# Dilated attention's projections: token order of the stationary operand and of the rows kept in DRAM

## The chip, the cores and the metric

The kernel runs on one core of a Trainium2 chip. The metric is the device time of one execution in microseconds. Three runs of the kernel before took 3687.85, 3690.18 and 3696.85 us, with a median of 3690.18 us.

## The reference

A first block (a modulated mixer with a bidirectional mLSTM and an MLP) is followed by a second block of two layers. The change lies in the second block. There, each layer normalises 1024 tokens of 1024 features, multiplies them by a wide matrix and feeds three branches: a recurrent mixer (RWKV), a sparse attention that chooses 256 keys for each query, and a dilated attention. The results go through an output matrix and a gated per-layer input. The dilated branch:

```python
DIL_WINDOWS = (128, 512, 2048)
DIL_RATES = (1, 4, 16)

def dilated_group(q, k, v, rate, steps):
    B, S, H, dh = q.shape
    n = S // rate
    to_res = lambda t: jnp.swapaxes(t.reshape(B, n, rate, H, dh), 1, 2).reshape(B * rate, n, H, dh)
    o, lse = banded_attention(to_res(q), to_res(k), to_res(v), steps)
    o = jnp.swapaxes(o.reshape(B, rate, n, H, dh), 1, 2).reshape(B, S, H, dh)
    lse = jnp.swapaxes(lse.reshape(B, rate, n, H), 1, 2).reshape(B, S, H)
    return o, lse

def dilated_branch(z, cos, sin):
    q, k, v, g = split_cols(z, DIL_COLS)
    q = partial_rope(heads(q), cos, sin)
    k = partial_rope(heads(k), cos, sin)
    for gi in range(DIL_GROUPS):          # two heads of 64 in each of three groups
        o, lse = dilated_group(q[:, :, hs], k[:, :, hs], v[:, :, hs], DIL_RATES[gi], DIL_WINDOWS[gi] // DIL_RATES[gi])
        ...
    alpha = jax.nn.softmax(jnp.stack(lses, axis=2), axis=2)
    return (o * alpha).reshape(B, S, DIL_WIDTH) * jax.nn.silu(g)
```

So group 0 attends over neighbouring tokens, group 1 over tokens of the same class modulo 4, and group 2 over tokens of the same class modulo 16.

## The kernel before

The second block works on half-layers of 512 tokens, (layer 0, half 0), (0, 1), (1, 0) and (1, 1). For each, `in2` (line 1159) makes the projections, `branches` (line 1077) runs the sparse and the dilated attention, and `rwkv` (line 1527) the recurrent mixer in three units per half.

All projections use `dense` (line 273). The normalised tokens lie feature-major in SBUF as eight tiles of 128 features x 512 tokens, each split into a high part `xh` and a low part `xl`. Weights stream in, 256 columns and two k tiles at a time: `chunk` (line 248) loads 256 KB, ScalarE rounds them to `wh` (line 254), GpSimd takes the rest as `wl` (line 255), with three buffers of each. Each product is three matmuls, `wh` with `xh`, `wh` with `xl` and `wl` with `xh` (line 287). Two kinds exist:

- `dense_a` (line 298) makes feature-major results. The weights are the stationary operand and 512 tokens the moving one.
- `dense_b` (line 305) makes token-major results. 128 tokens are the stationary operand and 256 weight columns the moving one. Two token tiles share a PSUM bank, and a group of 256 columns fills two banks.

`in2` has seven groups of the second kind (`tok`, line 1179). Groups 0 to 3 hold the sparse attention's columns and group 0 of the dilated attention. They take tokens in natural order (`nat`) and are stored in a DRAM tensor `zd` of 512 x 1024. Groups 4 to 6 hold the queries, keys and values of the dilated groups 1 and 2. They take every fourth token (`cls`, line 1175), so that one token tile is one class modulo 4, and are stored in a DRAM tensor `zc` of four classes x 128 rows x 768 columns. ScalarE copies each bank to SBUF (line 1182), and SyncE's queue stores it (line 1183). In half 0 the order of the groups is 0, 3, 1, index keys in the first unit of the recurrent mixer, 2 and 4 in the second, 5, 6 and the gates in the third. In half 1 it is 0, 3, 1, index keys ahead of all, then 2 and 4, then 6 and 5, then the gates.

The dilated attention (`dil`, line 1726) has 12 blocks in each half, 3 groups x 4. For groups 1 and 2 a block is one class. `dil_keys` (line 1750) loads its queries and keys `zq` (line 1768), its values `dv` (line 1770) and, in half 1, the values of the half before (line 1774). GpSimd rotates `zq` by a table that is laid out by class. Scores, values and statistics go out by `dil_rows` (line 1747), which for groups 1 and 2 picks every fourth row of a DRAM tensor; `ud` and `ml` are written that way (lines 1829 and 1805).

The sparse attention chooses its keys in `choose` (line 1665), 31 steps of a sign count on ScalarE (line 1687), a count and small updates on VectorE (lines 1689 to 1692), one behind the other. It runs for the row tiles from the third of a layer on. The attention of a row tile (`dsa_attend`, line 1612) ends in a product with its gate, loaded from DRAM (lines 1621 and 1662).

Nothing is ordered by hand on the engines. A planner puts the instructions of each engine in order by a simulated timeline and by priorities: `branches` comes first, the recurrent mixer second, the projections fill in. Each engine, and SyncE's queue of DMAs, then runs its own order. All DMAs are issued by SyncE.

Of the kernel before, what the change touches and what calls it, by code (L numbers as in the profile page):

```python
# [15 lines left out]
PSUM = bass.MemoryType.PSUM  # L16
# [179 lines left out]

class K:
# [36 lines left out]
    def f(self, name):  # L234
        """a scratch tile of 2 KB a partition"""
        return self.fp.tile([128, 516], F32, name=name, tag="f", bufs=4)
# [5 lines left out]
    def chunks(self, src, n):  # L242
        """a group of n weight columns, split exactly into two float32r parts, two k tiles at a time"""
        nc = self.nc
        for j in range(0, src.shape[1], 2):
            yield self.chunk(src, n, j)
# [11 lines left out]
    def narrow(self, src, xs, out):  # L258
        """feature-major products of 64 columns, with the weights' two parts side by side: those of the second part
        come out from partition 64 on"""  # L260
        nc = self.nc
# [11 lines left out]
    def dense(self, src, n, banks):  # L273
        """products with a streamed weight group. banks: lists, one per PSUM bank, of (out, xs, f), where f makes
        (lhsT, rhs) of the weights and x of a k tile. Only a bank's first product starts its sums."""
        last = src.shape[1] - 1
        for ch in self.chunks(src, n):
            self.products(ch, banks, 0, last)
# [14 lines left out]
    def tok_jobs(self, ps, xs, t0, pick=None):  # L293
        """two token tiles of 256 columns in one bank"""
        pick = pick or (lambda x, t: x[:, 128 * t:128 * t + 128])
        return [(ps[:, 256 * t:256 * t + 256], xs, lambda w, x, t=t0 + t: (pick(x, t), w)) for t in range(2)]

    def dense_a(self, src, n, xs):
        """feature-major products [columns, 512] of a group of n weight columns, one bank per 128"""
        out = [self.bank(self.dense_tag()) for _ in range(0, n, 128)]  # L300
        self.dense(src, n, [[self.col_jobs(ps[:min(128, n - 128 * c)], xs, 128 * c, min(128, n - 128 * c))]
                            for c, ps in enumerate(out)])
        return out

    def dense_b(self, src, xs, pick=None, n=2):
        """token-major products of a group of 256 weight columns: n banks [128, 2 token tiles, 256]"""
        out = [self.bank(self.dense_tag()) for _ in range(n)]
        self.dense(src, 256, [self.tok_jobs(ps, xs, 2 * c, pick) for c, ps in enumerate(out)])
        return out
# [8 lines left out]
    def rsqrt(self, dst, v, n, tag=""):  # L318
        """dst = v ** -0.5 for small tiles, by Newton from a bit-level seed"""
# [13 lines left out]
    def ln_stats(self, src, eps):  # L333
        """src [128, 1024] -> (mean, rstd, -mean*rstd) columns"""
# [13 lines left out]
    def halves(self, n, pool=None, bufs=8):  # L348
        """the high and low parts of eight k tiles of n columns"""
# [5 lines left out]
    def make_xt(self, tiles, scale, bias=None, pool=None, tag="pt"):  # L355
        """normalised token tiles -> feature-major hi/lo parts, scaled and shifted per feature"""
# [92 lines left out]
    def ada_a(self, w0):  # L449
        nc, I = self.nc, self.I  # L450
        cT = self.v1["cT"]
        # silu(c) = (tanh(c/2) + 1) * c/2
# [6 lines left out]
        # 16 columns of each condition  # L459
# [13 lines left out]
    def ada_weights(self, g, pool=None):  # L473
        """the rows of a group of 256 modulation columns, by k"""
# [7 lines left out]
    def ada_rows(self, ps, g, pool):  # L482
        """256 columns: four partial sums over k, on 32 partitions each"""
# [4 lines left out]
    def ada_pair(self, g, pool=None):  # L488
        """feature-major shifts and scales of 512 columns; scales have their +1 in the bias"""
# [13 lines left out]
    def ada_row(self, dst, g0, g):  # L503
        """dst [128, 1024]: a column group of the modulation, the same in every partition"""
# [19 lines left out]
    def conv(self, j, raw, n, out):  # L524
        """taps over raw[:, 0:n+2], silu"""
# [10 lines left out]
    def inproj_a(self, h, tiles, ctiles=None):  # L536
        """q, k (convolved), values and gates of the context and of half 0; of half 1 the gates only"""
# [74 lines left out]
    def spread(self):  # L612
        """a piece of the modulation that later steps need"""
# [3 lines left out]
    def sg_prep(self):  # L617
        """weights of the spatial gating and its per-token offsets"""
# [12 lines left out]
    def uvo(self, h):  # L631
        """spatial gating branch and output gate of half h, kept in DRAM"""
# [41 lines left out]
    def gates(self):  # L674
        """mLSTM gate fields; rows 0..3 run forward, rows 32..35 backward (in flipped order)"""
# [75 lines left out]
    def mlstm_a(self):  # L751
        """states at the start of every latent chunk, both directions"""
# [31 lines left out]
    def mlstm_b(self):  # L784
        nc, pm, C = self.nc, self.pm, self.Cst
        H = []
        for l in range(8):
# [14 lines left out]
            for d in range(2):  # L802
# [10 lines left out]
                # weights are at most one where they count  # L813
# [38 lines left out]
            # head norm, output gate  # L852
# [28 lines left out]
    def load_yt(self, h, pool, th, tl, bufs):  # L881
        """the two mixer halves, feature-major, in hi/lo parts"""
# [19 lines left out]
    def deepnorm(self, z):  # L902
        """layer norm of a token tile [128, 1024], in place"""
# [76 lines left out]
    def consts2(self):  # L980
        """constants and vectors of block 2"""
# [6 lines left out]
        # 0, 1 and -1, and very low numbers  # L988
# [33 lines left out]
    def block2(self):  # L1022
# [16 lines left out]
        self.zd, self.zc, self.gd = d("zd", [512, 1024]), d("zc", [4, 128, 768]), d("gd", [5, 128, 512])  # L1039
# [37 lines left out]
    def branches(self, i, h):  # L1077
        """sparse and dilated attention of a half: a row tile's choice of keys runs beside the attention of the one before"""
# [27 lines left out]
    def square(self, x, out, ss):  # L1106
        """ss = sums of the squares of x"""
        self.nc.scalar.activation(out, x, AF.Square, accum_out=ss)

    def sums(self):  # L1110
        """room for the sums of squares of up to four token tiles, by groups of 256 columns"""
        return self.sm.tile([128, 4, 4], F32, name="rms_ss")

    def rms(self, ss, n):
        """[128, n]: 1 / (root mean square) of n token tiles"""
# [8 lines left out]
    def shift(self, i, j, ps, z):  # L1124
        """token-shift mix of one column tile"""
# [8 lines left out]
    def gate_out(self, i, h, j, ps):  # L1134
        """2 * silu of a gate tile, kept in DRAM"""
# [6 lines left out]
    def in2_prep(self, i, X, tag="pd", ss=None):  # L1142
        """the normalised rows of four token tiles, feature-major"""
# [15 lines left out]
    def in2(self, i, h, X, xs=None):  # L1159
# [14 lines left out]
        nat = lambda x, t: x[:, 128 * t:128 * t + 128]  # L1174
        cls = lambda x, j: x.rearrange("p (n j) -> p j n", j=4)[:, j]
        zd = self.zd[i, h].rearrange("(c t p) n -> c p t n", c=2, t=2)
        zc = self.zc[i, h].rearrange("(c t) p n -> c p t n", c=2)

        def tok(g, dst, pick, o):
            for c, ps in enumerate(self.dense_b(I["w2B"][i, g], xs, pick)):  # L1180
# [16 lines left out]
        def gates(g):  # L1197
            for c, ps in enumerate(self.dense_a(A[7 + g], 256, xs)):
                self.gate_out(i, h, 2 * g + c, ps)

        first = [lambda: tok(0, zd, nat, 0), lambda: tok(3, zd, nat, 256), lambda: tok(1, zd, nat, 768), index_keys]
        t2, t4, t5, t6 = (lambda: tok(2, zd, nat, 512), lambda: tok(4, zc, cls, 0), lambda: tok(5, zc, cls, 256),
                          lambda: tok(6, zc, cls, 512))
# [21 lines left out]
    def rope(self, x, heads, width, name, t):  # L1225
        """rotate the first 16 (or 8) columns of every head in place; x [128, heads * width]"""
# [14 lines left out]
    def rwkv_a(self, i, h, p, wd, zr, zk, zv, zg):  # L1241
        """six heads by pairs: head j of a pair lies on partitions 64 j to 64 j + 63. Decay, keys and rates of a pair"""
# [11 lines left out]
        # by chunks: rates, keys, and the second head's rates again  # L1254
# [8 lines left out]
        # normalised keys  # L1263
# [26 lines left out]
    def rwkv_b(self, i, h, p, PC, P, kk, BK, zr, kp, zv, zg):  # L1290
        """chunk products, and inverses of the unit lower triangles, by doubling"""
# [3 lines left out]
        # own: a head's partitions, other: its neighbour's  # L1295
# [11 lines left out]
        def products(q):  # L1307
            """of four chunks, by heads: rates and keys against A and R. Rates end up on the head's own partitions."""
# [25 lines left out]
        def token_major(q):  # L1334
            """of four chunks: minus the rates, and the keys"""
# [17 lines left out]
        # rows against U on a head's own partitions, against V on the other ones  # L1353
# [24 lines left out]
        # of T the first block of 32 is left to do  # L1378
# [11 lines left out]
        # the last level, by its blocks  # L1390
# [16 lines left out]
    def inverse16(self, L, T, TT):  # L1407
        """the blocks of 16 on the diagonals of the unit lower triangles inverted (T; TT is its transpose), by doubling.
        Through DRAM a block comes onto one partition."""
# [14 lines left out]
        def part(x, w, r, c):  # L1424
            """the quarters (r, c) of the diagonal blocks of 2 w of x [64, 16, 16]: [64, blocks, w, w]"""
# [3 lines left out]
        # the blocks' strict upper parts fill up; Y[:, 1] is the transpose  # L1429
# [24 lines left out]
    def rwkv_c(self, i, h, p, PC, AR, XB, YB, TT, W, KB, bv, sg):  # L1454
        """the chain over chunks, then group norm, bonus and gate"""
        nc = self.nc
        Z = self.layer[i]["Z"][p]
        # of the very last pair, the outputs of the first tokens don't wait for the others
# [4 lines left out]
        for c in range(8):  # L1463
            cs = slice(c * 64, c * 64 + 64)
            pz = self.bank("pc", 1)
            # a head's rows of W: the state, then U
# [30 lines left out]
    def rwkv_y(self, i, h, p, py, bv, sg, t0, t1, tag):  # L1497
        """group norm, bonus and gate of some chunks; the mean is out already"""
# [28 lines left out]
    def rwkv(self, *unit):  # L1527
        """the first part of a pair and the rest of the one before; without a pair the rest only"""
# [6 lines left out]
    def dsa_scores(self, i, h, t):  # L1535
        """keys and index scores of a row tile of 128; where all keys before a query count, 0 for these, else very low"""
# [18 lines left out]
        # queries: high and low parts against the high parts of keys; high against low  # L1555
# [16 lines left out]
        # indexer rows: high, low, high parts against high, high, low  # L1572
# [16 lines left out]
        # index scores  # L1589
# [22 lines left out]
    def dsa_attend(self, i, h, t, qT, acc):  # L1612
        """attention of a row tile over its chosen keys"""
# [51 lines left out]
    def choose(self, x, n):  # L1665
        """x [128, n] scores -> 0 for the 256 greatest of each row (of equal ones the first), -2^103 for the others.
# [334 lines left out]
```

## Time and profile before

| | |
|---|---|
| median of three runs | 3690.18 us |
| span of the profiled execution | 3684.1 us |
| TensorE matmul busy | 3446.7 us (94%), 24036 instructions |
| TensorE weight loads busy | 2953.4 us (80%) |
| VectorE busy | 2124.3 us (58%) |
| ScalarE busy | 1745.5 us (47%) |
| GpSimd busy | 1344.0 us (36%) |
| DMA | 376.61 MB, mean 102 GB/s |

The page gives no second time for the profiled execution, only its span from the first to the last instruction; the median of the runs is 6.1 us above that span. In the profile PE is TensorE's matmul, PEld its weight load, DVE is VectorE, ACT is ScalarE, POOL is GpSimd and SP is SyncE; a `q` behind the name is the engine's own queue of instructions that are not counted as busy. Matmuls are pipelined, so that the records of two of them overlap; the distance between two starts says how fast they follow.

### The profile page before, as it was taken

Reading aid. Unit: us, or ns where it says so; the run is one execution under the profiler, and the core shown is the slowest. Engines: PE = TensorE matmul, PEld = TensorE weight load, DVE = VectorE, ACT = ScalarE, POOL = GpSimd, SP = SyncE. Lnnn points to the kernel's source line nnn. Section 1 sums busy time; section 2 is a strip of 40 time slices with the busy share of each in tenths; the row PEclk is TensorE's granted clock in tenths of the full one; section 3 lists DMA queues with packets and bytes.
Section 4 is the critical chain, followed back from the end, with each engine's and each line's share of the span. In section 5 each row is a group of like instructions: output and inputs, shape, how many; then the busy total and the mean of one; then the engine's idle time right before and its main releaser. Section 6 shows DMA issues by size and latency. Waiting matters only on the chain. (4 is left out here: it accounts for less than half of the span.)

```text
span 3684.1 us, 66369 instructions
## 1 busy us (share of the span) xinstructions
PE 3446.7 (94%) x24036; PEld 2953.4 (80%) x24036; DVE 2124.3 (58%) x6359; ACT 1745.5 (47%) x3976; POOL 1344.0 (36%) x1331
## 2 busy tenths in 40 slices
PE   7989898999999989999999999899999999899897
PEld 5968787999899978887787787688888878688776
DVE  6277858112711264436655898872357555778974
ACT  3244334333333333337635666553357545557654
POOL 1333345444644463322322232233232233133245
PEclk8999998999999999998998899799999999899899
DMA  5433352222322233223321322332233432132434
GB/s 219 130 100 118 124 184 82 95 97 95 107 95 95 96 126 101 79 81 106 107 77 54 106 75 61 117 90 83 71 113 82 135 96 80 48 112 64 129 120 142
DMA packets 322856, 376.61 MB, mean 102 GB/s; under 512 B 113376, under 2 KB 189408, under 8 KB 322528
## 3 DMA queue, kind: packets, MB, share of 16 engines
q1 hardware_dynamic: 322528, 372.37, 32.4%
q8 instruction: 189, 3.10, 0.3%
q14 instruction: 139, 1.14, 0.1%
HBM read 315.54 MB, written 56.72 MB: 101 GB/s over the span
## 5 line engine op out<-in xcount | busy, mean ns | idle before, releaser
L255 POOL TENSOR_TENSOR wl<-wf,wh 128x512 fp32r<-128x512 f32 x812 | 1084.2, 1338 | 1835.0 <-ACT wh L254 1698.8
L254 ACT ACTIVATE wh<-wf 128x512 fp32r<-128x512 f32 x812 | 508.4, 627 | 903.4 <-PE pd L287 388.1
L287 PE MATMUL pd<-wh,xh 128*128 128x256 f32 x2240 | 699.8, 314 | 22.3 <-ACT raw L567 6.6
L287 PE MATMUL pd<-wh,xl 128*128 128x256 f32 x2240 | 695.1, 311 | 0.0
L287 PE MATMUL pd<-wl,xh 128*128 128x256 f32 x2240 | 692.7, 312 | 2.5 <-POOL wl L255 2.1
L287 PEld LDWEIGHTS pd<-wh,xh 128*128 128x128 f32 x2240 | 485.0, 217 | 42.9 <-issue 9.4
L287 PEld LDWEIGHTS pd<-wl,xh 128*128 128x128 f32 x2240 | 484.0, 217 | 16.4 <-issue 6.1
L287 PEld LDWEIGHTS pd<-wh,xl 128*128 128x128 f32 x2240 | 487.1, 217 | 9.9 <-issue 1.2
L287 PE MATMUL pd<-xh,wh 128*128 128x512 f32 x896 | 372.9, 417 | 28.8 <-DVE tg L1139 17.3
L287 PE MATMUL pd<-xl,wh 128*128 128x512 f32 x896 | 363.9, 406 | 0.2 <-DVE xl L371 0.2
L287 PE MATMUL pd<-xh,wl 128*128 128x512 f32 x896 | 352.7, 407 | 0.1
L1687 ACT ACTIVATE junk<-acc,t_nt 128x384 bf16<-128x384 f32 (+3 forms) x372 | 257.1, 691 | 145.7 <-DVE t_nt L1692 115.2
L287 PEld LDWEIGHTS pd<-xh,wh 128*128 128x128 f32 x896 | 175.4, 196 | 73.1 <-DVE tg L1139 18.3
L287 PEld LDWEIGHTS pd<-xl,wh 128*128 128x128 f32 x896 | 175.1, 195 | 39.3 <-issue 3.9
L287 PEld LDWEIGHTS pd<-xh,wl 128*128 128x128 f32 x896 | 174.2, 194 | 39.7 <-issue 1.7
L954 DVE CAST hh<-f 128x512 fp32r<-128x512 f32 x64 | 54.1, 845 | 243.2 <-ACT f L951 243.2
L1689 DVE TENSOR_SCALAR_CACHE_REDUCE junk<-acc,t_nt 128x384 bf16<-128x384 f32 (+2 forms) x186 | 125.5, 675 | 3.6
L1603 DVE SCALAR_TENSOR_TENSOR acc<-r,iw,acc 128x512 f32<-128x512 f32 (+3 forms) x140 | 102.8, 734 | 34.4 <-ACT r L1598 32.1
L1691 DVE TENSOR_SCALAR t_dec<-t_s,t_kb 128x1 int32<-128x1 f32 x372 | 77.8, 209 | 69.1 <-ACT junk L1687 64.7
L287 PE MATMUL pd<-wh,hh 128*128 128x256 f32 x384 | 108.7, 283 | 3.3 <-DVE y L923 3.3
L287 PE MATMUL pa<-wl,hh 128*128 128x256 f32 x384 | 108.0, 284 | 3.4 <-POOL wl L255 3.4
L287 PE MATMUL pb<-wh,hh 128*128 128x256 f32 x384 | 109.3, 285 | 0.2 <-ACT wh L254 0.2
(555 smaller groups left out, 7881.0 us busy)
## 6 DMA issues: line engine op xcount, KB each, us to landing
wf<-in_w_dram SPq DMA_DIRECT2D x256, 256.0 KB, 3.0
wf<-in_w2A_dram SPq DMA_DIRECT2D x144, 256.0 KB, 3.2
wf<-in_w2B_dram SPq DMA_DIRECT2D x112, 256.0 KB, 3.1
wf<-in_w_in_dram SPq DMA_DIRECT2D x80, 256.0 KB, 3.1
wf<-in_w2o_dram SPq DMA_DIRECT2D x80, 256.0 KB, 3.2
wf<-in_w2g_dram SPq DMA_DIRECT2D x80, 256.0 KB, 3.1
wa<-in_w_ada_dram SPq DMA_DIRECT2D x32, 512.0 KB, 5.1
X<-x_d SPq DMA_DIRECT2D x20, 512.0 KB, 5.1
```

Of the source, the lines that this page charges most:

```text
L254: nc.scalar.activation(wh, wf, AF.Copy)
L255: nc.gpsimd.tensor_sub(wl, wf, wh.bitcast(F32))
L287: self.nc.tensor.matmul(out, lhsT, rhs, start=k == first and j == 0 and q == 0, stop=k == last and j == len(bank) - 1 and q == 2)
L954: nc.vector.tensor_copy(hh, f)
L1603: nc.vector.scalar_tensor_tensor(a, r[:, :n], iw[:, hd:hd + 1], a, op0=OP.mult, op1=OP.add)
L1687: nc.scalar.activation(junk[:, :m], x[:, :m], AF.Sign, scale=-1.0, bias=nt, accum_out=s)
L1689: ts(junk[:, m:], x[:, m:], nt, 0.0, op0=OP.is_le, op1=OP.add, accum_out=c0)
L1691: ts(dec, s, kb, 2.0 ** b, op0=OP.is_lt, op1=OP.mult)
```

## The change

`tok_jobs` and `dense_b` lose their `pick`, and all seven groups take tokens in natural order. `zc` becomes 512 rows x 768 columns in natural order. `dil_keys` picks its class from it when it loads, by `dil_rows`, as every fourth row. The rest of the diff takes out comments and docstrings.

```diff
-    def tok_jobs(self, ps, xs, t0, pick=None):
-        pick = pick or (lambda x, t: x[:, 128 * t:128 * t + 128])
-        return [(ps[:, 256 * t:256 * t + 256], xs, lambda w, x, t=t0 + t: (pick(x, t), w)) for t in range(2)]
+    def tok_jobs(self, ps, xs, t0):
+        return [(ps[:, 256 * t:256 * t + 256], xs, lambda w, x, t=t0 + t: (x[:, 128 * t:128 * t + 128], w))
+                for t in range(2)]
...
-        self.dense(src, 256, [self.tok_jobs(ps, xs, 2 * c, pick) for c, ps in enumerate(out)])
+        self.dense(src, 256, [self.tok_jobs(ps, xs, 2 * c) for c, ps in enumerate(out)])
...
-        self.zd, self.zc, self.gd = d("zd", [512, 1024]), d("zc", [4, 128, 768]), d("gd", [5, 128, 512])
+        self.zd, self.zc, self.gd = d("zd", [512, 1024]), d("zc", [512, 768]), d("gd", [5, 128, 512])
...
-        nat = lambda x, t: x[:, 128 * t:128 * t + 128]
-        cls = lambda x, j: x.rearrange("p (n j) -> p j n", j=4)[:, j]
-        zd = self.zd[i, h].rearrange("(c t p) n -> c p t n", c=2, t=2)
-        zc = self.zc[i, h].rearrange("(c t) p n -> c p t n", c=2)
-
-        def tok(g, dst, pick, o):
-            for c, ps in enumerate(self.dense_b(I["w2B"][i, g], xs, pick)):
+        zd, zc = (z[i, h].rearrange("(c t p) n -> c p t n", c=2, t=2) for z in (self.zd, self.zc))
+
+        def tok(g, dst, o):
+            for c, ps in enumerate(self.dense_b(I["w2B"][i, g], xs)):
...
-        t2, t4, t5, t6 = (lambda: tok(2, zd, nat, 512), lambda: tok(4, zc, cls, 0), lambda: tok(5, zc, cls, 256),
-                          lambda: tok(6, zc, cls, 512))
+        t2, t4, t5, t6 = (lambda: tok(2, zd, 512), lambda: tok(4, zc, 0), lambda: tok(5, zc, 256),
+                          lambda: tok(6, zc, 512))
...
-        zd, zc, ti = self.zd[i, h], self.zc[i, h], 4 * h + j
+        zd, ti = self.zd[i, h], 4 * h + j
+        zc = self.dil_rows(g, j, self.zc[i, h])
...
-            nc.sync.dma_start(zq, zc[j][:, 256 * g - 256:256 * g])
+            nc.sync.dma_start(zq, zc[:, 256 * g - 256:256 * g])
...
-            nc.sync.dma_start(dv[:, 1], zc[j][:, vs])
+            nc.sync.dma_start(dv[:, 1], zc[:, vs])
...
-                nc.sync.dma_start(dv[:, 0], self.zc[i, 0][j][:, vs])
+                nc.sync.dma_start(dv[:, 0], self.dil_rows(g, j, self.zc[i, 0])[:, vs])
```

## Rows read from the trace of the kernel before

**Rows 1.** The page's first part: span, busy time by engine.
```profile
span 3684.1 us, 66369 instructions
PE 3446.7 (94%) x24036; PEld 2953.4 (80%) x24036; DVE 2124.3 (58%) x6359; ACT 1745.5 (47%) x3976; POOL 1344.0 (36%) x1331
```

**Rows 2.** DMA issues: out<-in, count, KB each, median us to landing.
```profile
zc<-s SPq DMA_DIRECT2D x24, 256.0 KB, 2.2
...
zq<-zc SPq DMA_DIRECT2D x32, 128.0 KB, 2.1
...
ud<-dod SPq DMA_DIRECT2D x48, 64.0 KB, 1.7
dv<-zc SPq DMA_DIRECT2D x48, 64.0 KB, 1.9
```

**Rows 3.** Timeline of PE (start us, us, instruction), a group with every fourth token.
```profile
1600.06 0.39 PE L287 MATMUL pd<-wh,xh 128*128 128x256 f32 x1
...
1605.89 0.39 PE L287 MATMUL pd<-wh,xl 128*128 128x256 f32 x1
```

**Rows 4.** Timeline of PE, a group in natural order.
```profile
2924.09 0.28 PE L287 MATMUL pd<-wl,xh 128*128 128x256 f32 x1
...
2927.08 0.28 PE L287 MATMUL pd<-wh,xh 128*128 128x256 f32 x1
```

**Rows 5.** Timeline of PEld, the group with every fourth token.
```profile
1600.16 0.33 PEld L287 LDWEIGHTS pd<-wh,xl 128*128 128x128 f32 x1
```

**Rows 6.** Timeline of PEld, the group in natural order.
```profile
2924.21 0.19 PEld L287 LDWEIGHTS pd<-wh,xl 128*128 128x128 f32 x1
```

**Rows 7.** Windows: stretch, us, busy by engine, granted clock, DMA share, GB/s.
```profile
1500.00:1627.00 127.00, 123.21 (x769) 108.92 (x770) 38.07 (x132) 40.14 (x100) 35.81 (x55) 0.97 0.28 76
1848.00:1979.00 131.00, 130.35 (x816) 111.22 (x817) 56.99 (x156) 49.21 (x104) 30.26 (x36) 0.96 0.23 66
2540.00:2666.00 126.00, 121.13 (x790) 107.57 (x790) 40.76 (x134) 41.31 (x103) 35.42 (x55) 0.99 0.26 74
3030.00:3156.00 126.00, 126.00 (x779) 111.25 (x780) 68.85 (x239) 70.14 (x171) 37.79 (x58) 0.99 0.28 75
1375.00:1505.00 130.00, 124.63 (x963) 106.63 (x961) 56.28 (x147) 45.73 (x88) 51.27 (x63) 0.99 0.34 102
1600.00:1606.00 6.00, 6.00 (x27) 6.00 (x28) 0.00 (x0) 1.12 (x2) 1.28 (x1) 1.00 0.57 125
2924.00:2951.00 27.00, 27.00 (x228) 27.00 (x227) 4.05 (x4) 10.04 (x18) 14.17 (x16) 1.00 0.46 146
```

**Rows 8.** Timeline of DVE: first gated attention of a half, and its wait.
```profile
1648.32 0.29 DVE L1662 SCALAR_TENSOR_TENSOR ya<-da,ga 128x128 f32<-128x128 f32 x1 [1.74 <-DMA ga<-gd]
...
2684.80 0.29 DVE L1662 SCALAR_TENSOR_TENSOR ya<-da,ga 128x128 f32<-128x128 f32 x1 [0.81 <-DMA ga<-gd]
```

**Rows 9.** Timeline of DVE: first and last steps of choices of keys.
```profile
1981.98 0.81 DVE L1675 TENSOR_SCALAR_CACHE_REDUCE junk<-acc 128x640 bf16<-128x640 f32 x1
...
2065.35 0.80 DVE L1711 TENSOR_TENSOR acc<-acc,junk 128x640 f32<-128x640 f32 x1
...
3016.39 0.81 DVE L1675 TENSOR_SCALAR_CACHE_REDUCE junk<-acc 128x640 bf16<-128x640 f32 x1
...
3126.29 0.83 DVE L1711 TENSOR_TENSOR acc<-acc,junk 128x640 f32<-128x640 f32 x1
...
3238.07 1.91 DVE L1711 TENSOR_TENSOR acc<-acc,junk 128x768 f32<-128x768 f32 x1
```

**Rows 10.** Waits of POOL from 1500 to 3160 us: us, times, longest.
```profile
POOL ro L1235 <- DMA zq<-zc: 88.7, 23, 7.9
```

**Rows 11.** Timeline of SP: two stores of a group and a load between.
```profile
3121.64 0.37 SPq L1183 DMA_DIRECT2D zc<-s  x1
...
3124.29 0.38 SPq L1770 DMA_DIRECT2D dv<-zc  x1
...
3128.54 0.42 SPq L1183 DMA_DIRECT2D zc<-s  x1
```

More of the change, by code (lines that the diff above doesn't have):

```diff
@@ L303, in dense_a, with dense_b @@
         return out
-    def dense_b(self, src, xs, pick=None, n=2):
+    def dense_b(self, src, xs, n=2):
         out = [self.bank(self.dense_tag()) for _ in range(n)]
-        self.dense(src, 256, [self.tok_jobs(ps, xs, 2 * c, pick) for c, ps in enumerate(out)])
+        self.dense(src, 256, [self.tok_jobs(ps, xs, 2 * c) for c, ps in enumerate(out)])
         return out
@@ L1199, in gates @@
                 self.gate_out(i, h, 2 * g + c, ps)
-        first = [lambda: tok(0, zd, nat, 0), lambda: tok(3, zd, nat, 256), lambda: tok(1, zd, nat, 768), index_keys]
-        t2, t4, t5, t6 = (lambda: tok(2, zd, nat, 512), lambda: tok(4, zc, cls, 0), lambda: tok(5, zc, cls, 256),
-                          lambda: tok(6, zc, cls, 512))
+        first = [lambda: tok(0, zd, 0), lambda: tok(3, zd, 256), lambda: tok(1, zd, 768), index_keys]
+        t2, t4, t5, t6 = (lambda: tok(2, zd, 512), lambda: tok(4, zc, 0), lambda: tok(5, zc, 256),
+                          lambda: tok(6, zc, 512))
         g0, g1 = lambda: gates(0), lambda: gates(1)
```

## The prediction

> **What bounds the kernel now.** I read the page's busy shares first, then the stores and loads of `zc` in the DMA view, then TensorE's timeline inside and outside the three groups that the change touches, then the busy time of the stretches that hold these groups, and last what the scalar and vector engines were doing just behind each stretch. The page shows TensorE busy 3446.7 of 3684.1 us and VectorE 2124.3 [rows 1]. A busy share of 94% is an average, so the question is what TensorE does in the stretches of the change. `zc` is stored 24 times, once for each PSUM bank of the three groups in four half-layers [rows 2]. One bank is 2 token tiles x 8 k tiles x 3 products = 48 matmuls, so 24 x 48 = 1152 matmuls take every fourth token as their stationary operand.
>
> In one of these groups matmuls start at 1600.06 and, 25 starts later, at 1605.89: 5.83 / 25 = 0.2332 us each [rows 3]. In a group of the same kind with tokens in natural order, 25 starts take 2927.08 - 2924.09 = 2.99 us: 0.1196 us each [rows 4]. Both have 128 stationary and 256 moving columns. The weight load takes 0.33 us in the first and 0.19 us in the second [rows 5, 6]. The clock does not explain it: it was granted in full, 1.00, that is 2.4 GHz, in both stretches [rows 7]. Nor does a wait: the strided stretch has TensorE busy 6.00 of 6.00 us with VectorE at zero [rows 7]. What differs is the step of the loaded operand.
>
> The Trainium skill speaks against this reading. In "TensorE: Matmul & The Clock Gate", section "LDWEIGHTS (loading the stationary operand)", the load's time follows from its number of columns alone, and section "Step-by-step: what each phase is for" lets it run beside the matmul before. By these two the step would cost nothing and the sum below would be zero. The trace disagrees: the same 128 columns take 0.33 against 0.19 us, and the starts move apart with them [rows 3 to 6].
>
> The four stretches that hold the groups, each up to its last store of `zc`, are 1500 to 1627, 1848 to 1979, 2540 to 2666 and 3030 to 3156 us. TensorE is busy 123.21 of 127, 130.35 of 131, 121.13 of 126 and 126.00 of 126 us there; VectorE has 38.07, 56.99, 40.76 and 68.85 us of work [rows 7]. TensorE is the bound in all four.
>
> **The change, part by part.** *Stationary operand in natural order.* 1152 matmuls go from 0.2332 to 0.1196 us: 0.1136 us each, 32.7 us a half-layer (288 matmuls), 130.9 us of TensorE's time in all. The weights must then arrive twice as fast. They can: the natural-order stretch 2924 to 2951 ran 228 matmuls in 27.00 us, with TensorE never idle, ScalarE at 10.04 and GpSimd at 14.17 us [rows 7]; the same loads and splits feed the changed groups. Nothing else on TensorE is added or removed.
>
> How much of 32.7 us reaches the end differs by half-layer.
> - Layer 0, half 0: behind the three groups TensorE does the gates, and the first row tile's attention waits for a gate at 1648.32 [rows 8]. The choice of keys that follows starts later still. So all that comes after hangs on TensorE's stream. In a stretch with natural-order groups TensorE was busy 124.63 of 130 us [rows 7], 4.1% idle, where the strided one has 3.0%. I take 31 us, 1.7 under the full term, for waits that come up between.
> - Layer 0, half 1: TensorE has 0.65 us of slack in 131 and the long choice of keys starts at 1981.98, just behind the last strided group [rows 7, 9]. 31 us.
> - Layer 1, half 0: as the first, with the gate's wait at 2684.80 [rows 8], and 4.87 us of idle time already in 126 [rows 7]. 30 us.
> - Layer 1, half 1: here the choice of keys had begun at 3016.39, before the groups, and runs as two choices in a row to 3238.07 [rows 9]. It is a chain of ScalarE and VectorE steps, so faster matmuls help it only where VectorE, which works in order, stood behind a TensorE product. Its bounds are 0 and 32.7 us. The first of these choices took 3016.39 to 3126.29, 109.9 us, where the one of the same width in layer 0 took 1981.98 to 2065.35, 83.4 us [rows 9]. 26.5 us longer: some part of that is waiting for TensorE. I take the middle of the bounds, 16 us.
>
> Sum: 31 + 31 + 30 + 16 = 108 us.
>
> *Stores.* A bank's store has the same rows, 1 KB each, at the same addresses (four blocks of 128 rows in a row either way); only which token a row holds differs. 0 us.
>
> *Loads of every fourth row.* 32 loads of `zq` and 48 of `dv` keep their row lengths (1 KB and 512 B) but step 12 KB instead of 3 KB. No load in the trace does just that. The nearest is the store of `ud`, of which 32 in 48 write every fourth row of 512 B: median 1.7 us to landing, against 2.1 for `zq` and 1.9 for `dv` now [rows 2]. From that row a step of four rows costs nothing, and a gain in a load is not in sight either. Upper end: 1 us each for all 80, about half a load again, with nothing hidden, 80 us. Between 1500 and 3160 us GpSimd already stands 88.7 us before its rotation for `zq` [rows 10], off the path while TensorE binds. I take 0, by the nearest row.
>
> *A wait that is added.* A class lay in the rows of one store, so a block waited for one bank; now it waits for both. Layer 1, half 1 shows the most: stores at 3121.64 and 3128.54, and a load of values between them at 3124.29 [rows 11]. That load would go after 3128.54 plus 2.2 us to landing [rows 2], 6.5 us later. SyncE issues in order, so behind it stand the weight loads of the next groups, and TensorE waits for those once the three weight buffers are used up. Bounds: 0 to 6.5 us a half-layer, 26 us in all. Later blocks read long after both stores. I take 0: the second bank's last 12 matmuls come right behind the first bank's, and at 0.1196 us each the two stores move closer together.
>
> *Same tables.* The rotation keeps its table by class; the rest of the edit is names and comments: 0 us.
>
> The profiled span, 3684.1 us, lies 6.1 us under the median of 3690.18, which I take for what lies around it. 3684.1 - 108 + 6.1 = 3582 us.
>
> **The rivals.**
> *Other chains take over.* VectorE and the recurrent mixer's small matmuls may not keep up once the dense work is a quarter shorter. For it: VectorE has 68.85 us in the fourth stretch, and 126 - 32.7 = 93 us leaves little room in an in-order queue. Against it: 38 to 57 us in the other three [rows 7]. With half of the first three terms and nothing of the fourth the gain is 46 us: 3644 us. Point from which it decides: where TensorE's idle share in those stretches goes past a fifth.
>
> *The whole term arrives.* If the fourth half also hangs on TensorE, because its choices were waiting behind strided products, 130.9 us: 3559 us. The 26.5 us speak for it; that two choices of keys span the whole stretch speaks against it.
>
> *It does nothing.* The load's step would not be the cause, and the changed groups keep 0.2332 us: 3690 us. Against it stands that the two groups differ in nothing else that the rows show. This is what the rule of the Trainium skill's "TensorE: Matmul & The Clock Gate", section "LDWEIGHTS (loading the stationary operand)", would make of the change.
>
> *Slower: scattered rows.* The loads of `zq` and `dv` are the one thing made worse. At 80 loads the gain of 108 us is eaten at 1.35 us more for each, if all stand on the path: `zq` at 3.5 us instead of 2.1. At 2 us more, with all of it exposed, 160 - 108 = 52 us slower: 3742 us. The row of `ud` speaks against it, and so do the stretches in which TensorE binds, whatever a block waits for.
>
> **How the numbers follow.** Forecast (3565 to 3605): 0.62. Other chains take over: 0.19. The whole term: 0.13. Nothing: 0.03. Scattered rows: 0.03. The likeliest is 3582. The range reaches down past the third case, to which shorter waits elsewhere may add, and up into the second until about a third of it is inside: 3545 to 3640, which leaves out some 0.19. A change of 0.3%, 11 us, is about what can be told from none. The first three cases are all faster by more: 0.94; same 0.03; slower 0.03.
>
> **What would show it.** In the profile after: the weight loads of the three groups at 0.19 us and starts 0.12 us apart at full clock; TensorE's busy time down by about 130 us; the first gate's wait some 31 us earlier and the first long choice of layer 0 some 62 us earlier; the last choices only about 108 us earlier. `zq` landing above 3 us, or a wait of TensorE for weights behind a load of `dv`, would show the fourth rival or the added wait. Strided-looking starts of 0.23 us would make the whole prediction wrong; a fourth half that moves by 30 us, or by none, makes only its size wrong.

## The result, and the profile after

Four runs of the changed kernel took 3552.55 to 3571.42 us, with a median of 3558.84 us against 3690.18 us: a ratio of 0.966, interval 0.964 to 0.968. That is 131.3 us less. The forecast had been 3582 us, between 3565 and 3605. The measured time lies under that and is the one of the rival in which the whole term arrives, 3559 us, which had been given a chance of 0.13.

The page's first part of the kernel after, to be held against [rows 1]:

```profile
span 3554.0 us, 66371 instructions
...
PE 3321.5 (93%) x24036; PEld 2825.4 (79%) x24036; DVE 2129.1 (60%) x6359; ACT 1743.3 (49%) x3976; POOL 1354.3 (38%) x1331
```

The same 24036 matmuls keep TensorE busy 125.2 us less, its weight loads take 128.0 us less, and the other engines' sums hardly move. The span fell by 130.1 us. The run that left this profile took 3555.7 us, 1.7 us more than its span.

PE's timeline of the group that [rows 3] showed, in the kernel after (start us, us, instruction):

```profile
1575.06 0.28 PE L287 MATMUL pd<-wh,xh 128*128 128x256 f32 x1
...
1578.06 0.28 PE L287 MATMUL pd<-wh,xl 128*128 128x256 f32 x1
```

and one weight load of it, from the same kernel's timeline of the loads:

```profile
1575.07 0.19 PEld L287 LDWEIGHTS pd<-wh,xl 128*128 128x128 f32 x1
```

Between these two matmuls lie 25 starts: 3.00 / 25 = 0.120 us each, where it had been 0.233 us [rows 3], and the load takes 0.19 us, as in the natural group before [rows 6].

The next two fences cut both spans at the same six instructions: the gate waits of [rows 8], and the starts and ends of choices of [rows 9]. Each row is one such interval with the busy time of each engine. First the kernel before (start:end, length, then PE, PEld, DVE, ACT, POOL busy with their instructions, granted clock, DMA share, GB/s):

```profile
0.00:1648.32 1648.32, 1547.70 (x10438) 1365.57 (x10439) 758.81 (x1993) 593.57 (x1049) 714.99 (x586) 0.96 0.34 113
1648.32:1981.98 333.66, 316.21 (x2146) 260.89 (x2145) 196.28 (x632) 181.21 (x462) 96.31 (x126) 0.93 0.32 91
1981.98:2684.80 702.82, 671.02 (x4742) 549.62 (x4741) 499.39 (x1603) 389.13 (x962) 202.24 (x260) 0.93 0.28 84
2684.80:3016.39 331.59, 309.47 (x2336) 265.91 (x2336) 194.15 (x634) 198.29 (x527) 106.87 (x132) 0.95 0.35 106
3016.39:3238.07 221.68, 208.01 (x1256) 174.18 (x1254) 148.27 (x518) 121.73 (x296) 60.84 (x75) 0.93 0.26 70
3238.07:3684.10 446.03, 394.28 (x3126) 337.23 (x3126) 327.37 (x985) 261.54 (x680) 162.74 (x153) 0.93 0.37 114
```

Then the kernel after:

```profile
0.00:1613.09 1613.09, 1515.07 (x10438) 1332.27 (x10439) 756.82 (x1994) 593.03 (x1049) 715.71 (x586) 0.97 0.35 115
1613.09:1913.00 299.91, 280.11 (x2147) 225.65 (x2146) 198.27 (x632) 180.12 (x462) 97.58 (x126) 0.95 0.36 102
1913.00:2583.19 670.19, 639.88 (x4742) 517.47 (x4741) 499.38 (x1602) 388.50 (x962) 204.81 (x260) 0.92 0.30 88
2583.19:2914.20 331.01, 310.30 (x2336) 266.55 (x2335) 193.53 (x634) 198.12 (x527) 107.06 (x132) 0.94 0.36 106
2914.20:3105.50 191.30, 175.94 (x1256) 141.28 (x1254) 152.91 (x518) 120.51 (x296) 63.96 (x74) 0.93 0.29 79
3105.50:3554.00 448.50, 400.16 (x3126) 342.17 (x3126) 328.16 (x985) 263.02 (x681) 165.19 (x153) 0.91 0.37 114
```

The number of matmuls in each interval is the same to one, so the intervals hold the same work. Four of them hold the strided groups of one half-layer each. Subtracting row by row:

| interval with the groups of | length | TensorE busy | TensorE idle |
|---|---|---|---|
| layer 0, half 0 (first row) | -35.2 | -32.6 | -2.6 |
| layer 0, half 1 (second) | -33.8 | -36.1 | +2.4 |
| layer 1, half 0 (third) | -32.6 | -31.1 | -1.5 |
| none (fourth) | -0.6 | +0.8 | -1.4 |
| layer 1, half 1 (fifth) | -30.4 | -32.1 | +1.7 |
| none (sixth) | +2.5 | +5.9 | -3.4 |

TensorE's busy time falls by 131.9 us in the four, beside 130.9 us worked out from the starts of two groups, and almost all of it is length that disappears. The fifth row is the one that the forecast had at 16 us. The last row has nothing of the change in it: the same 3126 matmuls took 5.9 us longer at a mean granted clock of 0.91 instead of 0.93 (1.00 is 2.4 GHz, and the lower level is 1.2 GHz), and the row is 2.5 us longer. The first experiment below shows that this is no price of the time saved.

In the fifth interval the two choices of keys of [rows 9] run one behind the other. VectorE's timeline after, the first instruction of each choice and the last:

```profile
2914.20 0.81 DVE L1672 TENSOR_SCALAR_CACHE_REDUCE junk<-acc 128x640 bf16<-128x640 f32 x1
...
3006.93 0.83 DVE L1708 TENSOR_TENSOR acc<-acc,junk 128x640 f32<-128x640 f32 x1
...
3007.80 0.95 DVE L1672 TENSOR_SCALAR_CACHE_REDUCE junk<-acc 128x768 bf16<-128x768 f32 x1
...
3105.50 0.95 DVE L1708 TENSOR_TENSOR acc<-acc,junk 128x768 f32<-128x768 f32 x1
```

They take 92.7 and 97.7 us, where they took 3126.29 - 3016.39 = 109.9 us, and about 111 us from there to 3238.07 [rows 9]. No step of a choice was touched, but both became shorter, by 17 and 13 us. The waits of VectorE in this interval show where that comes from. The longest of its waits for a product of TensorE, before and then after (waiting tile and line <- releaser: us in total, times, longest):

```profile
DVE ch_x L1472 <- PE pc L1468: 9.2, 6, 2.9
```

```profile
DVE ch_x L1469 <- PE pc L1465: 2.7, 3, 2.1
```

All its waits for products of TensorE sum to 30.1 us before and 6.3 us after. They are small products of the recurrent mixer and of the attentions, which stand in TensorE's order among the projections' matmuls: in 18.9 of the 30.1 us TensorE was at work on the projections.

The stores of `zc` and the loads that now pick every fourth row, in the list of DMA issues of the kernel after, beside [rows 2]:

```profile
zc<-s SPq DMA_DIRECT2D x24, 256.0 KB, 3.2
...
zq<-zc SPq DMA_DIRECT2D x32, 128.0 KB, 2.4
...
dv<-zc SPq DMA_DIRECT2D x48, 64.0 KB, 1.9
```

`zq` lands 0.3 us later, `dv` as before. The stores land 1.0 us later, which the forecast did not have.

The instructions of TensorE, VectorE, ScalarE and GpSimd stand in the same order in both kernels. On SyncE alone, three loads of values moved: two behind the second store of their bank pair, one, which already stood behind it, behind the next weight load.

### The profile page after: what moved, and what is told of

The parts are those of the page before. It is cut to its first block, busy times and chain, and to the rows that moved or that the text cites. A ratio compares the mean times of both kernels' runs of the same rounds, so it can differ in the third digit from the quotient of the medians.

```text
span 3554.0 us, 66371 instructions
## 1 busy us (share of the span) xinstructions
PE 3321.5 (93%) x24036; PEld 2825.4 (79%) x24036; DVE 2129.1 (60%) x6359; ACT 1743.3 (49%) x3976; POOL 1354.3 (38%) x1331
## 5 line engine op out<-in xcount | busy, mean ns | idle before, releaser
L287 PE MATMUL pd<-wh,xh 128*128 128x256 f32 x2240 | 654.2, 294 | 21.4 <-ACT raw L567 6.6
L287 PE MATMUL pd<-wh,xl 128*128 128x256 f32 x2240 | 650.9, 292 | 0.1
L287 PE MATMUL pd<-wl,xh 128*128 128x256 f32 x2240 | 648.5, 292 | 1.4 <-POOL wl L255 0.9
L287 PEld LDWEIGHTS pd<-wh,xh 128*128 128x128 f32 x2240 | 432.8, 194 | 41.6 <-issue 8.7
L287 PEld LDWEIGHTS pd<-wl,xh 128*128 128x128 f32 x2240 | 431.6, 194 | 14.7 <-issue 5.4
L287 PEld LDWEIGHTS pd<-wh,xl 128*128 128x128 f32 x2240 | 434.1, 194 | 10.3 <-issue 1.2
L287 PE MATMUL pa<-wh,hh 128*128 128x256 f32 x384 | 109.0, 285 | 0.0
```

The lines of the kernel that those rows point to most:

```text
L287: self.nc.tensor.matmul(out, lhsT, rhs, start=k == first and j == 0 and q == 0, stop=k == last and j == len(bank) - 1 and q == 2)
```

## Experiments

Three questions were open: whether the matmuls' step is the cause, and not the loads or the order of `zc`; why a half-layer in which two choices of keys fill the time follows TensorE all the same; and what it is in the step that costs. In all the runs the instructions of TensorE, VectorE, ScalarE and GpSimd stand in the order of the changed kernel. SyncE's order is that of the kernel before in the first run and, but for layer 1, half 1, in the second, so the added wait is not in them there; in the others it is that of the changed kernel. The kernel before took a median of 3687.04 us beside the first four experiments.

**The new loads alone.** The three groups take every fourth token again; the stores put each class's rows back to their natural places in `zc`, and the loads pick every fourth row.

```diff
+        cls = (lambda x, j: x.rearrange("p (n j) -> p j n", j=4)[:, j]) if True else None
+        if cls:
+            zc = self.zc[i, h].rearrange("(n c t) w -> c n t w", c=2, t=2)
...
-            for c, ps in enumerate(self.dense_b(I["w2B"][i, g], xs)):
+            for c, ps in enumerate(self.dense_b(I["w2B"][i, g], xs, pick=cls if g > 3 else None)):
```

> The matmuls of the three groups take every fourth token again in all four half-layers, and each bank is stored with every fourth row, so that zc lies in natural order and the loads of zq and dv pick every fourth row as in the changed kernel. The load part of the change alone. Theory T (all of the gain is TensorE's time, from the step of the stationary operand): 3690 us, ratio to the kernel before 1.000 within 0.003; starts of the groups' matmuls 0.233 us apart. Rival L (the 23 us of gain above the forecast came from the order of the rows in DRAM): 3667 us, ratio 0.994. Rival S (scattered rows cost something that the faster matmuls hid): above 3700 us, ratio over 1.003, with zq landing above 3 us.

Measured: 3686.37 us, ratio 0.9999, interval 0.9987 to 1.001. Scattered rows, on the store's side as well, cost nothing that can be measured (the interval is some 4 us to either side), and they gain nothing. So the gain comes with the matmuls' operand. The profiled run took 3682.38 us with a span of 3680.6, 1.8 us around it. The stores of `zc` land after 2.2 us in it, as before; 3.2 us show in the kernel after and in the four others below in which all three groups take natural order.

The last interval of this kernel, cut as the sixth row above, from the last instruction of the second of the two choices to the end:

```profile
3229.95:3680.60 450.65, 400.13 (x3126) 341.30 (x3126) 326.41 (x985) 261.73 (x681) 163.94 (x153) 0.91 0.36 113
```

Nothing was saved on TensorE here, and yet these 3126 matmuls took 400.1 us at 0.91, as in the kernel after. So the 5.9 us between the kernels before and after are no answer of the clock to the time saved.

**The change in layer 1, half 1 alone.** As the experiment before, with the strided groups in the other three half-layers only.

```diff
+        cls = (lambda x, j: x.rearrange("p (n j) -> p j n", j=4)[:, j]) if (i, h) != (1, 1) else None
```

> Natural order only in layer 1, half 1, where the prediction took 16 us of 32.7; the other three half-layers take every fourth token and store every fourth row. Theory T (TensorE's stream passes its time on also beside the choice of keys, since VectorE and ScalarE stand in order behind its products): 30 us less than before, 3660 us, ratio 0.992; the two choices there end some 30 us earlier. Rival C (the choices of keys bind there, as the prediction had it, and the rest of the gain came from the other three): 3674 us, ratio 0.996, or 3690 us if they bind alone.

Measured: 3655.73 us, ratio 0.9914, interval 0.9897 to 0.9931; 31.3 us less than before by the medians. VectorE's timeline of this kernel, the ends of the two choices:

```profile
3002.95 0.81 DVE L1676 TENSOR_SCALAR_CACHE_REDUCE junk<-acc 128x640 bf16<-128x640 f32 x1
...
3095.80 0.83 DVE L1712 TENSOR_TENSOR acc<-acc,junk 128x640 f32<-128x640 f32 x1
...
3096.66 0.95 DVE L1676 TENSOR_SCALAR_CACHE_REDUCE junk<-acc 128x768 bf16<-128x768 f32 x1
...
3194.00 2.05 DVE L1712 TENSOR_TENSOR acc<-acc,junk 128x768 f32<-128x768 f32 x1
```

92.9 and 97.3 us, as in the full change. And the interval as one row of the windows of this kernel:

```profile
3002.95:3194.00 191.05, 175.46 (x1256) 140.94 (x1254) 152.56 (x518) 120.82 (x296) 64.52 (x75) 0.93 0.29 80
```

It is 30.6 us shorter than the fifth interval of the kernel before, with TensorE's busy time 32.6 us less. The 16 us that the forecast gave to this half-layer fall: it gives about 31 us, by itself and whatever the three others do.

**More TensorE time beside a choice, in layer 0.** The changed kernel, with the 384 matmuls of the output matrix of layer 0, half 0 strided (they run while half 1's second choice does). At 0.1136 us each that puts 43.6 us back on TensorE, and leaves all else.

```diff
-            for c, ps in enumerate(self.dense_b(self.I["w2o"][i, g], ys, n=nt // 2)):
+            for c, ps in enumerate(self.dense_b(self.I["w2o"][i, g], ys, n=nt // 2, pick=(lambda x, j: x.rearrange("p (n j) -> p j n", j=4)[:, j]) if (i, h) == (0, 0) else None)):
```

> The changed kernel, with the four groups of the output matrix of layer 0, half 0, given every fourth token as stationary operand (rows of that half are permuted, so the result differs): 4 groups x 96 = 384 matmuls at 0.1136 us more, 43.6 us of TensorE's time put into the stretch in which the long choices of keys run (VectorE 407 of 467 us busy there before). Theory T (TensorE passes on its time there as well, since it never runs out of work): 3559 + 44 = 3603 us, ratio to the kernel before 0.976. Rival C (the chain of choices covers it): 3559 to 3570 us, ratio 0.964 to 0.967.

Measured: 3597.29 us, ratio to before 0.9763, interval 0.9748 to 0.9778; 38.5 us over the changed kernel by the medians. The four runs of the changed kernel lie up to 19 us apart, so 38.5 us cannot be told from 43.6. The window of the second choice of layer 0, from the start of its first instruction on VectorE to the end of its last; first this kernel, then the changed one:

```profile
1996.72:2157.66 160.94, 159.16 (x913) 140.48 (x911) 105.82 (x341) 77.52 (x205) 34.24 (x32) 0.95 0.25 76
```

```profile
1999.69:2117.09 117.40, 114.43 (x912) 95.15 (x911) 108.41 (x341) 76.23 (x207) 35.92 (x32) 0.99 0.34 104
```

160.9 us instead of 117.4: 43.5 us longer, all that was put on TensorE. In the changed kernel VectorE has 108 us of work in these 117 us, and one would call the choice bound by VectorE. But with the same work it took 161 us as soon as TensorE had 159 us. The waits show how that happens. VectorE's waits in that choice, first in this kernel (waiting tile and line <- releaser: us in total, times, longest), then in the changed one:

```profile
DVE X L1900 <- PE pd L287: 12.2, 8, 2.9
...
DVE t_s L1687 <- ACT junk L1684: 8.0, 11, 5.1
...
DVE ch_z L1482 <- PE pc L1475: 7.1, 4, 2.6
```

```profile
DVE t_s L1687 <- ACT junk L1684: 3.3, 7, 2.1
...
DVE X L1900 <- PE pd L287: 0.3, 1, 0.3
```

Between the steps of the choice (`t_s`) VectorE has to take the output matrix's products out of PSUM (`X`) and the recurrent mixer's (`ch_z`). It works in order, so it stands there until TensorE has made them, 12.2 us instead of 0.3 at line 1900 alone, and the choice's next step stands behind.

**The same in layer 1.** The output matrix of layer 1, half 0, which runs ahead of the third choice of half 1 and beside it.

```diff
+            for c, ps in enumerate(self.dense_b(self.I["w2o"][i, g], ys, n=nt // 2, pick=(lambda x, j: x.rearrange("p (n j) -> p j n", j=4)[:, j]) if (i, h) == (1, 0) else None)):
```

> As the run before, but with the output matrix of layer 1, half 0, which runs beside the last two choices of keys, with nothing but the tail of the last half behind them: again 43.6 us of TensorE's time (rows of that half permuted). Theory T: 3603 us, ratio 0.976. Rival C (the last choices and the tail set the end, and TensorE's added time lies beside them): 3559 to 3575 us, ratio 0.964 to 0.969.

Measured: 3600.62 us, ratio to before 0.9765, interval 0.975 to 0.9781; 42 us over the changed kernel by the medians. The window of the third choice, here and in the changed kernel:

```profile
3182.00:3348.00 166.00, 158.17 (x1118) 140.42 (x1119) 119.34 (x386) 90.61 (x242) 41.21 (x50) 0.94 0.21 59
```

```profile
3160.00:3297.00 137.00, 131.04 (x1118) 113.60 (x1117) 120.67 (x386) 90.56 (x245) 42.05 (x50) 0.96 0.25 71
```

With 1118 matmuls in both and 120 us of work on VectorE, 29 us longer where TensorE has 27 us more. The other strided matmuls run ahead of this choice, from the end of the second choice to the start of the third, which takes 71.4 us, with TensorE busy in 71.3 of them, instead of 53.5. Nearly all 43.6 us arrive at the end in a third place.

**Which steps cost.** The changed kernel with steps of two, three and four tokens in groups 4, 5 and 6 of every half-layer. The values that they take to `zc` are of other tokens, and with a step of three some tokens twice.

```diff
+        two = lambda x, t: x.rearrange("p (h n j) -> p h j n", h=2, j=2)[:, t // 2, t % 2]
+        three = lambda x, t: x[:, :384].rearrange("p (n j) -> p j n", j=3)[:, t % 3]
+        four = lambda x, t: x.rearrange("p (n j) -> p j n", j=4)[:, t]
+        step = {4: two, 5: three, 6: four}
...
+            for c, ps in enumerate(self.dense_b(I["w2B"][i, g], xs, pick=step.get(g))):
```

> The changed kernel with three different steps of the stationary operand in the three groups, all in the same run: group 4 takes every second token (8 bytes apart), group 5 every third (12 bytes), group 6 every fourth (16 bytes); which tokens a row holds is then wrong, the count of matmuls is the same. Read from the distance of the starts at full clock. Theory line (a load is slowed by the number of 16-byte pieces that it touches, 32, 64, 96 and 128 for steps 1 to 4): step 4 at 0.233 us, step 3 near 0.175 us, step 2 at 0.120 us, hidden by the matmul. Rival any (any step but 1 costs the same): all three at 0.233 us. Rival whole (only pieces that share nothing are slow): steps 2 and 3 at 0.120 us. Time: by line 3559 + 384 x (0.055 + 0.1136) = 3624 us; by any 3690 us; by whole 3602 us.

Measured in one run: 3629.61 us, beside 3682.26 us for the kernel before. The 17 runs of the kernel before beside the first four experiments reach from 3679.89 to 3696.60 us, so in this run and the next two the distance of the starts decides, not the time. PE's timeline of this kernel in the three groups, at a granted clock of 1.00 (2.4 GHz) in each; pairs of rows, for steps of two, three and four:

```profile
1509.75 0.28 PE L287 MATMUL pd<-wh,xl 128*128 128x256 f32 x1
...
1511.31 0.28 PE L287 MATMUL pd<-wl,xh 128*128 128x256 f32 x1
...
1576.54 0.33 PE L287 MATMUL pd<-wl,xh 128*128 128x256 f32 x1
...
1578.64 0.34 PE L287 MATMUL pd<-wl,xh 128*128 128x256 f32 x1
...
1594.69 0.40 PE L287 MATMUL pd<-wl,xh 128*128 128x256 f32 x1
...
1597.25 0.40 PE L287 MATMUL pd<-wh,xl 128*128 128x256 f32 x1
```

13 starts in 1.56 us, 12 in 2.10 and 11 in 2.56: 0.120, 0.175 and 0.233 us a matmul. One weight load of each:

```profile
1508.44 0.20 PEld L287 LDWEIGHTS pd<-wl,xh 128*128 128x128 f32 x1
...
1574.01 0.26 PEld L287 LDWEIGHTS pd<-wh,xh 128*128 128x128 f32 x1
...
1595.25 0.33 PEld L287 LDWEIGHTS pd<-wl,xh 128*128 128x128 f32 x1
```

128 fp32 values at steps of 8, 12 and 16 bytes touch 64, 96 and 128 pieces of 16 bytes. 0.175 / 96 and 0.233 / 128 are both 1.82 ns a piece; by that 64 pieces would take 0.117 us, an estimate, which is hidden under the matmul's own 0.120. So a step of two costs nothing here, and four costs no more than three in proportion. Up to a step of four the pieces grow as the step does, so that it is the pieces that count, and not the distance itself, is not shown: a step of eight, with 128 pieces too, was not run. The Trainium skill's "SBUF — State Buffer", section "Specifications (TRN2)", says that memory there is read in lines of 16 bytes, and that at least two hits in a line are needed for full speed. These steps agree: two values in a piece at a step of two take 0.120 us, one at a step of four 0.233. The moving operand of the next two runs does not: at a step of two it has two in each piece and takes 0.451 us instead of 0.227.

**A step on the moving operand.** The changed kernel, with the 512 moving tokens of the gates taken class by class: classes modulo four in the first group of gates, modulo two in the second. So the gates stand in another order of tokens.

```diff
+        return (ps, xs, lambda w, x: (w[:, c:c + m], x.rearrange("p (n j) -> p j n", j=by) if by > 1 else x))
...
-            for c, ps in enumerate(self.dense_a(A[7 + g], 256, xs)):
+            for c, ps in enumerate(self.dense_a(A[7 + g], 256, xs, (4, 2)[g])):
```

> The changed kernel with a step on the moving operand instead: the two gate groups, 512 moving columns a matmul, stream the tokens by fours (first group, 16 bytes apart) and by twos (second group, 8 bytes); their columns are then permuted. 192 matmuls each. Theory port (a read of SBUF by TensorE is slowed by a step whichever operand it is): the first group's starts go from 0.225 to 512 x 0.233 / 128 = 0.93 us apart, 192 x 0.7 = 135 us more, 3690 us or more. Rival load (only the weight load suffers): 0.225 us apart and 3559 us.

Measured in one run: 3632.81 us, beside 3682.26 us for the kernel before. PE's timeline of this kernel, the first group and then the second, at a granted clock of 1.00:

```profile
1599.46 0.64 PE L287 MATMUL pd<-xh,wl 128*128 128x512 f32 x1
...
1603.61 0.64 PE L287 MATMUL pd<-xh,wh 128*128 128x512 f32 x1
...
1629.44 0.63 PE L287 MATMUL pd<-xh,wh 128*128 128x512 f32 x1
...
1633.95 0.63 PE L287 MATMUL pd<-xl,wh 128*128 128x512 f32 x1
```

The first group in the changed kernel, also at 1.00:

```profile
1595.10 0.39 PE L287 MATMUL pd<-xl,wh 128*128 128x512 f32 x1
...
1597.37 0.39 PE L287 MATMUL pd<-xh,wh 128*128 128x512 f32 x1
```

9 starts in 4.15 us and 10 in 4.51: 0.461 and 0.451 us, twice the 0.227 us of natural order (10 starts in 2.27 us). Neither expectation held: not 1.82 ns a piece, which for 512 pieces would be 0.93 us, and not a cost on the load's side alone.

**Is it the order, or how much of a piece is used?** The first group of gates takes its moving tokens in whole blocks of 128 neighbours, in another order; the second takes pairs of neighbours, every other pair, so that half of each 16 bytes is used.

```diff
+        blocks = lambda x: x.rearrange("p (a b n) -> p b a n", a=2, b=2)
+        pairs = lambda x: x.rearrange("p (n j k) -> p j n k", j=2, k=2)
...
+            for c, ps in enumerate(self.dense_a(A[7 + g], 256, xs, (blocks, pairs)[g])):
```

> A control to the run with a step on the moving operand. The first gate group streams four blocks of 128 neighbouring tokens in another order (no step, but a pattern of two dimensions), the second streams pairs of neighbouring tokens, one pair in two (8 bytes together, then 8 left out); columns are permuted. Theory step (single elements with a gap are slow, whatever the gap): blocks at 0.23 us a matmul, pairs at 0.23 us, 3559 us. Rival pattern (any moving operand that is not one run is slow): both at 0.45 us, 3559 + 384 x 0.22 = 3644 us. Rival bytes (a piece of 16 bytes half used is slow): blocks 0.23 us, pairs 0.45 us, 3601 us.

Measured in one run: 3593.75 us, beside 3688.13 us for the kernel before. PE's timeline of this kernel, blocks and then pairs:

```profile
1599.68 0.39 PE L287 MATMUL pd<-xh,wh 128*128 128x512 f32 x1
...
1600.59 0.39 PE L287 MATMUL pd<-xl,wh 128*128 128x512 f32 x1
...
1620.39 0.63 PE L287 MATMUL pd<-xh,wh 128*128 128x512 f32 x1
...
1623.55 0.63 PE L287 MATMUL pd<-xl,wh 128*128 128x512 f32 x1
```

4 starts in 0.91 us, 0.228 us each, and 7 in 3.16 us, 0.451 us each. Another order of whole blocks is free; runs of two neighbours, which use half of each piece, double the matmul. Whether the short run or the half-used piece is the cause is not told apart. Why a quarter-used piece (a step of four) costs no more than a half-used one on this side, where on the stationary side it costs twice as much, stays open.

## Why the prediction was right in its cause, and what it had wrong

- *The cause.* Right. The groups went from 0.233 to 0.120 us a matmul, and the loads of every fourth row alone give a ratio of 0.9999. The rule of the Trainium skill's "TensorE: Matmul & The Clock Gate", section "LDWEIGHTS (loading the stationary operand)", that a weight load's time follows from its columns alone falls with it: 128 columns took 0.19, 0.20, 0.26 or 0.33 us by their step, one to four.
- *The weights arrive in time.* Right: the interval rows show TensorE's idle time up by no more than 2.4 us in any half-layer.
- *The first three half-layers, 31, 31 and 30 us.* A little low: 35.2, 33.8 and 32.6. I had taken one or two us off for waits that come up between. TensorE's idle time went down by 2.6 us in the first, up by 2.4 in the second and down by 1.5 in the third. The second came out over 32.7 all the same, since TensorE's busy time fell by 36.1 us there, at a granted clock of 0.95 instead of 0.93.
- *The fourth half-layer, 16 us between 0 and 32.7.* This is the step that failed, in its mechanism and not in its size alone: it measured 30.4 us in the full change and 30.6 by itself. I had read two choices back to back as a chain with a length of its own, which faster matmuls help only in part, and had taken the middle for lack of a row that decides. The 26.5 us by which the first choice was longer than its like in layer 0 pointed the right way, but not at the size: 17.2 us of them came back, and 13.2 us more in the second choice. A choice is interleaved with other work that takes TensorE's products, in the fixed order of VectorE and ScalarE, and in a stretch where TensorE is 94% busy (208.01 of 221.68 us) these are what it waits for: VectorE 30.1 us before, 6.3 after. The choices shrink when TensorE's work goes (109.9 to 92.7 us) and stretch when it comes (117.4 to 160.9 us).
- *The stores, the loads and the tables at nothing.* Right in the time. But the stores land after 3.2 us instead of 2.2, and `zq` 0.3 us later; GpSimd's waits for `zq` sum to 95.9 us over the execution, where they were 100.6. What slows the stores was not tried. It shows in all the kernels whose three groups all run at 0.120 us a matmul, and not in the first experiment.
- *The added wait at nothing.* No trace of it in the time: two loads of values went behind a second store, one of them the case that I had priced, and its half-layer still gave 30.4 us. A kernel with this wait alone was not tried.
- *Other chains take over.* Not here. VectorE has 152.91 of 191.30 us in the fifth interval and still leaves room. But 108 of 117 us in a choice of layer 0 says that it is close; what a further cut of TensorE's work would bring in such a stretch was not tried.
- *The step from span to median.* Off by some 4 us: I took 6.1 us as lying around the span, and it is 1.7 to 1.8. The rest was a profiled execution quicker than the median. In the gain, 131.3 us by the medians and 130.1 by the spans, it cancels.

In sum: 108 us had been taken, and the intervals give 35.2 + 33.8 + 32.6 + 30.4 = 132.0 us. 14.4 of the 24 us between lie in the fourth half-layer, 4.2, 2.8 and 2.6 in the others, and 0.6 us gained and 2.5 us lost lie where nothing was changed. That the measured time still lies between the outer bounds, 3545 and 3640, is due to their being drawn past the rival that came true.

## What to carry to other kernels

When TensorE binds, look early at the step of each matmul operand: a step of four fp32 values on the stationary side nearly doubled a 128x256 matmul, a step of two on the moving side doubled a 128x512 one, and the reordering that the first served, done by the DMA in rows of 512 B or 1 KB, cost nothing that could be measured. When engines work in fixed orders that weave two chains together, don't price one chain as if it ran alone: ask which engine is never idle in the stretch, and expect its time to pass on nearly one for one, even through a chain of another engine that looks full (here 43.6 us put back gave 38.5 and 42). The check is cheap: put a known amount of time back on the suspected engine beside that chain, and see whether the chain stretches.

## What the runs showed of the hardware that was not expected

- The step of a load of 128 fp32 columns sets the pace of matmuls of 256 columns, once the load is the longer: 0.120, 0.120, 0.175 and 0.233 us for steps of one to four. The last two fit 1.82 ns for each 16-byte piece that is touched.
- On the moving side a step of two, a step of four, and pairs of neighbours all cost the same, 0.45 to 0.46 us instead of 0.227 for 512 columns; blocks of 128 neighbours in another order cost nothing.
- TensorE's granted clock differs between profiled executions without a cause in the matmuls: the same 3126 matmuls of the last interval were busy 394.3 us at 0.93 in the kernel before, 394.6 at 0.93 in the run with three steps, 400.1 at 0.91 in the run with the loads alone and 400.2 at 0.91 in the kernel after. Terms of a few us cannot be read from one profile of each kernel.
